# A stream-encoder step on one core: one half of a row factor summed one product later, and the last pair of heads' forms made on VectorE

## The chip, the cores and the metric

The kernel runs on one core of a Trainium2 chip, in one launch. The metric is device time in microseconds (us), the median of several executions. The engines have the profile's names: PE is TensorE (PEld its weight loads), DVE is VectorE, ACT is ScalarE, POOL is GpSimd, SP is SyncE. SP issues most of the DMA transfers; POOL and ACT issue some.

## The reference

One layer of an encoder runs on 512 prompt frames and 64 sample frames, 576 rows of width 2048. All of it is float32.

```python
hn = rmsnorm(x, g_norm1);  proj = hn @ w_in                 # 2048 -> 6144
q, k = rmsnorm per head;   o_attn = stick_breaking(q, k, v) # 8 heads of 128
u = gc * hc;  o_conv = gb * conv3_causal(u)                 # 1024 channels
mix = concat(rmsnorm(o_attn, g_attn_out), rmsnorm(o_conv, g_conv_out))
x = x + mix @ w_out
h2 = rmsnorm(x, g_norm2)
x = x + (silu(h2 @ w_gate) * (h2 @ w_up)) @ w_down          # 2048 -> 5632 -> 2048
```

## The kernel before

**Layout.** Activations lie with channels on the 128 partitions and the 576 frames along the row, in two halves of 288 (`HALVES`). A float32 operand is split into a rounded high part (a cast on ACT) and the rest (a subtraction on DVE, or on POOL where told so). `split` does both, at lines 222 and 223. A product of two such operands takes three matmuls, high by high, low by high, high by low, each 128x128 by 128x288.

**Products in sevens.** Most large products use seven block products in place of eight (numbered 1 to 7 in the code). Eight channel pairs and three matmuls make 24 matmuls for one block product. `prepare` makes the weight operand of a product four products ahead (a cast on ACT, a subtraction on DVE, and before it sums of weight blocks such as `s1`, written `s` in the profile, and differences in place in `raw_a` and `raw_b`). `multiply` issues the matmuls. `run` calls it and does what follows the product: `kept` copies a partial result out of PSUM on ACT while the same PSUM tile goes on collecting, and `finish` adds parts, multiplies by the row factor, and applies SiLU (gate) or the product with the gate (up).

**The feed-forward's start.** `order` lists the products. It begins

```python
order = [(0, 1), (0, 2), (1, 1), (1, 2), (0, 7), (0, 6), (0, 5), (0, 3), (0, 4), (1, 6), ...
```

with unit 0 the first gate block and unit 1 the first up block. Products 1, 6 and 3 of a unit collect in one PSUM tile, `psy`. After product 6 the copy `u2` is taken from it, and product 3 of the same unit must add to it only after that copy.

**The row factor.** RMSNorm's factor per frame, `R2`, is applied after the product, so the first products can start without it. The squares of the residual are summed over tiles in `acc2`; `split` makes `parts2`; `row_scale2` sums them over the partitions with two matmuls per half against a tile of ones (`channel_sums`, lines 470 and 471), and `rsqrt_mean` (lines 461 to 466) makes the factor with Ln and Exp on ACT and four steps on DVE. Its scratch tiles are shared: `ms` and `t` have one buffer each, and `kept` uses the same two tags, `ms` for the first copy of unit 1 and `t` for `u2`.

**The heads' forms.** The output projection's first units, for attention, take as frames seven combinations ("forms") of four blocks of a pair of heads. `head_forms` makes them for four pairs (k = 0 to 3): forms 1 to 3 are the blocks themselves, forms 5, 7, 6 and 4 are differences made in place on POOL (line 558). `put` splits each into one of eight stage tiles in turn and SP stores it. The low part of forms 5 and 6 is made on POOL, of the others on DVE. This is work in the background, stepped by `pipe.tick()` after each channel pair of a product; pairs 2 and 3 are the tile `o_ob`, the stage tiles are `hf`. It ends while the first products in sevens of the input projection begin (`conv_run`, line 1036, whose weights are `raw_a` and `raw_c`, whose evacuations are line 1060).

**Order of the work.** Each engine runs its own instructions in order. A scheduler decides that order when the program is built, from its own estimates; stretches of it are fixed by hand for some engines. So a change at one place can move instructions nearby on every engine.

Of the kernel before, what the change touches and what calls it, by code (L numbers as in the profile page):

```python
# [13 lines left out]
ALU = mybir.AluOpType  # L14
# [6 lines left out]
HALF = T // 2  # L21
HALVES = ((0, HALF), (HALF, T))
D = 2048
KD = D // P
NH = 8
# [69 lines left out]
def tile_hybrid_stream_step(  # L95
# [6 lines left out]
    nc = tc.nc  # L102
# [118 lines left out]
    def split(hi, lo, src, lo_eng=None):  # L221
        nc.scalar.copy(out=hi, in_=src)  # L222
        (lo_eng or nc.vector).tensor_tensor(out=lo, in0=src, in1=hi.bitcast(F32), op=ALU.subtract)  # L223

    def parts(name):
        t = tmp.tile([P, 2, HALF], F32R, tag="hl", name=name)
        return t[:, 0], t[:, 1]
# [32 lines left out]
    def misc(name):  # L260
        return ps_z.tile([P, 512], F32, tag="misc", name=name, bufs=2)
# [111 lines left out]
    with tc.manual_schedule(engines={mybir.EngineType.Activation, mybir.EngineType.DVE, mybir.EngineType.SP}):  # L373
# [26 lines left out]
        for kt in range(KD + LAG):  # L400
# [21 lines left out]
            if kt == 16:  # L422
                nc.vector.tensor_tensor(out=lo1[:, :1024], in0=raws[1][:, :1024], in1=hi1[:, :1024].bitcast(F32),  # L423
                                        op=ALU.subtract)
# [43 lines left out]
    def channel_sums(src_hi, src_lo, a, b, name):  # L468
        ps = misc(name)[:, : b - a]
        mm(ps, oner, src_hi, start=True, stop=False)  # L470
        mm(ps, oner, src_lo, start=False, stop=True)
        return ps
# [54 lines left out]
    def head_forms():  # L527

        turn = [0]
        two = [parts("sqg") for _ in HALVES]
        for (sh, sl), (a, b) in zip(two, HALVES):
            split(sh, sl, acc_a[:, a:b])
        yield 6
        for (sh, sl), (a, b) in zip(two, HALVES):
            rsqrt_mean(acc_a[:, a:b], channel_sums(sh, sl, a, b, "ssg"), 8 * P, HALF)
            yield 4
        for k in range(NH // 2):
            pair = o_half[k // 2][:, 2 * (k % 2) : 2 * (k % 2) + 2, :]  # L540
            four = pair.rearrange("p k (i t) -> p (k i) t", i=2)
            b11, b12, b21, b22 = (four[:, q, :] for q in range(4))
            for r in range(2):
                nc.vector.scalar_tensor_tensor(out=pair[:, r], in0=pair[:, r], scalar=col("ga", 2 * k + r), in1=acc_a,
                                               op0=ALU.mult, op1=ALU.mult)
            yield 2

            def put(f, src, lo_eng):
                t = bt["stage"][:, turn[0] % NP]
                turn[0] += 1  # L550
                split(t[:, 0], t[:, 1], src, lo_eng)
                nc.sync.dma_start(out=form_dram[f - 1, k].rearrange("f p t -> p f t"), in_=t.bitcast(F32))

            for f, src in ((1, b11), (2, b21), (3, b22)):
                put(f, src, nc.vector)
                yield 2
            for f, out, a, b in ((5, b11, b12, b11), (7, b12, b12, b22), (6, b22, b22, b11), (4, b21, b21, b22)):
                nc.gpsimd.tensor_tensor(out=out, in0=a, in1=b, op=ALU.subtract)
                yield 1
                put(f, out, nc.gpsimd if f in (5, 6) else nc.vector)  # L560
                yield 2
            if k == 1:
                bt["raw"] = apool.tile([P, 2048], F32, tag="oa", name="raw_c")
                assert cwanted[0] == (1, 0)
                call_columns([2])
# [970 lines left out]
    def run(n, p_):  # L1536
        st = unit[n]
        kind, fp = UNITS[n][:2]

        def kept(tag):  # L1540
            t = tmp.tile([P, HALF], F32, tag=tag, name="part", bufs=1)
            nc.scalar.copy(out=t, in_=st["y"])  # L1542
            return t

        def done(c, i, ps, part=None):
            if kind != "down":
                finish(kind, fp, c, i, ps, part)
            elif n in last:
                store_y(n, c, i)

        def add(c, i, ps, part=None):

            if kind != "down":
                return
            if n in first:
                if part is not None:
                    nc.vector.tensor_tensor(out=acc[fp, c, i], in0=ps, in1=part, op=ALU.add)
                else:
                    nc.scalar.copy(out=acc[fp, c, i], in_=ps)
                return  # L1560
            if ps is not None:
                nc.vector.tensor_tensor(out=acc[fp, c, i], in0=ps, in1=acc[fp, c, i], op=ALU.add)
            if part is not None:
                nc.gpsimd.tensor_tensor(out=acc[fp, c, i], in0=acc[fp, c, i], in1=part, op=ALU.add)

        if kind == "down" and p_ == 1 and n in first:
            take_blocks(fp)
        later = n not in first
        if p_ == 1:
            st["y"] = ps_pj.tile([P, HALF], F32, tag="pj", name="psy")  # L1570
            multiply(st["y"], n, 1, True)
            st["p1"] = kept("ms" if n else "acc")
        elif p_ == 2:
            x = misc("psx3")[:, :HALF] if n == 1 else ps_z.tile([P, 512], F32, tag="z0", name="psx2")[:, :HALF]
            multiply(x, n, 2, True)
            if n == 0:
                row_scale2()
            add(0, 0, x, st["p1"])
            done(0, 0, x, st["p1"])
        elif p_ == 6:  # L1580
            multiply(st["y"], n, 6, False)
            st["u2"] = kept("ms" if n == NGU - 1 else "t")
            if later:
                add(1, 0, None, st["u2"])
        elif p_ == 7:
            st["w"] = ps_z.tile([P, 512], F32, tag=f"z{n % 2 + 1}", name="psw")[:, :HALF]
            multiply(st["w"], n, 7, True)
            if later:
                add(1, 1, st["w"])
        elif p_ == 5 and n == 0:  # L1590

            x = misc("psx5")[:, :HALF]
            multiply(x, n, 5, True)
            st["p5"] = tmp.tile([P, HALF], F32, tag="acc", name="part5", bufs=1)
            nc.scalar.copy(out=st["p5"], in_=x)
            u4 = tmp.tile([P, HALF], F32, tag="ms", name="part", bufs=1)
            nc.gpsimd.tensor_tensor(out=u4, in0=st["p5"], in1=st["u2"], op=ALU.add)
            done(1, 1, st["w"], u4)
        elif p_ == 5:
            multiply(st["y"], n, 5, False)  # L1600
            u4 = kept("acc")
            add(1, 1, None if later else st["w"], u4)
            done(1, 1, st["w"], u4)
        elif p_ == 3:
            multiply(st["y"], n, 3, False)
            add(0, 1, st["y"])
            done(0, 1, st["y"], st.get("p5"))
        else:
            multiply(st["w"], n, 4, False)
            add(1, 0, st["w"], None if later else st["u2"])  # L1610
            done(1, 0, st["w"], st["u2"])
# [3 lines left out]
    first, last = {v[0] for v in visits.values()}, {v[-1] for v in visits.values()}  # L1615
# [166 lines left out]
    R2 = rpool.tile([P, T], F32, tag="R", name="R2", bufs=2)  # L1782
    parts2 = []
# [2 lines left out]
        split(sh, sl, acc2[i])  # L1786
        parts2.append((sh, sl))

    def row_scale2():
        for i, (a, b) in enumerate(HALVES):  # L1790
            ss = channel_sums(*parts2[i], a, b, "ss2")
            rsqrt_mean(R2[:, a:b], ss, D, HALF)

    for k_ in range(2, AHEAD):
        prepare(*order[k_])
    for k_, (n, p_) in enumerate(order):
        if (n, p_) == (NGU - 1, 1):
            hold.append(True)
            mode.enter_context(tc.manual_schedule(engines={mybir.EngineType.Activation, mybir.EngineType.DVE,
                                                           mybir.EngineType.SP, mybir.EngineType.Pool}))  # L1800
        run(n, p_)
        if k_ + AHEAD < len(order):
            prepare(*order[k_ + AHEAD])
        if k_ == 2:
            for t, j0, j1 in zip(late["b22"], (1, 0), (NP, 1)):
                nc.sync.dma_start(out=t.bitcast(F32), in_=b22_dram[j0:j1].rearrange("j f p t -> p (j f) t"))
        for p in turned.get((n, p_), ()):
            if p == "w":
                load_columns(one=True)
            else:  # L1810
                load_pair(p)
        if (n, p_) == (NGU - 1, 4):
            pairs.append(6)
            since = -16
            hold.clear()
            load_columns()
        if n >= NGU:
            pairs += calls[n - NGU] if p_ == 4 else ()
            since += UNITS[n][3]
            if pairs and since >= PACE:  # L1820
                load_pair(pairs.pop(0))
                since = 0
        if p_ == 2:
            for d in residual.get(n, ()):
                add_residual(d)
# [39 lines left out]
```

## Time and profile before

| what | value |
|---|---|
| time, median of 3 | 2369.54 us (2368.44 to 2373.28) |
| profiled execution | 2369.07 us, its span 2367.0 us |
| granted TensorE clock | 1.00 |
| PE busy | 99% of the span |
| DVE, ACT, POOL busy | 82%, 49%, 12% |

The profile has several views. The page gives busy time by engine. The waits say who waited for whom. The timeline lists instructions in order: start in us from the span's start, length in us, engine, line, operation, output<-inputs, sizes, how many were merged (xN), and in brackets the idle time before and who ended it. The chain is the work that ended last, followed backwards.

### The profile page before, as it was taken

To read this page: it belongs to the slowest core of one execution; us is meant where nothing else is said; L and a number is where in the kernel's file an instruction comes from. 1 tells how busy PE (TensorE), PEld (TensorE's weight loads), DVE (VectorE), ACT (ScalarE), POOL (GpSimd) and SP (SyncE) were. 2 spreads that over 40 slices of the span, in tenths; PEclk is the share of its full clock that TensorE was granted. 3 is DMA by queue.
4 is the path that set the end of the run, shared out by engine and by line. 5 is a ranking of instruction groups with operands and counts; after the bars stand their busy time and mean duration, and the time that the engine had idled before them with its cause. 6 is when DMAs were issued, how large, how long until landed. Compare 5 with 4: busy or idle time off the path is not lost.

```text
span 2367.0 us, 43888 instructions
## 1 busy us (share of the span) xinstructions
PE 2340.9 (99%) x17581; PEld 2329.5 (98%) x17581; DVE 1935.3 (82%) x2908; ACT 1156.0 (49%) x2039; POOL 294.5 (12%) x386
## 2 busy tenths in 40 slices
PE   8999999999999999999999999999999999999998
PEld 8999999999999999999999999999999999999998
DVE  7878777788887889888888888888888777887896
ACT  6656655444444555444444444444444444444443
POOL 1011111341111230000000000000000002431221
PEclk9999999999999999999999999999999999999999
DMA  8466544684368654444444444444444936885553
GB/s 259 128 175 169 139 138 112 217 266 126 110 226 227 194 166 154 137 152 136 139 152 135 140 152 134 141 152 133 142 152 132 356 115 208 221 235 199 190 143 85
DMA packets 588804, 395.74 MB, mean 167 GB/s; under 512 B 100030, under 2 KB 577720, under 8 KB 588600
## 3 DMA queue, kind: packets, MB, share of 16 engines
q1 hardware_dynamic: 574776, 375.93, 50.9%
q0 software_dynamic: 8624, 16.22, 3.4%
q8 instruction: 137, 2.24, 0.4%
q10 hardware_dynamic: 5200, 0.79, 0.2%
q14 instruction: 67, 0.55, 0.1%
HBM read 301.45 MB, written 91.44 MB: 166 GB/s over the span
## 4 chain that ended last, share of the span: by engine, by line
PE 89%; DVE 5%; DMA 2%; ACT 2%; issue 1%; POOL 0%; ACTq 0%; SPq 0%; POOLq 0%; DVEq 0%
PE psy L1532 33%; PE psw L1532 16%; PE pj L213 13%; PE psx L1532 8%; PE psy L1036 6%; PE pjo L213 4%; PE psw L1036 3%; PE psx L1036 2%; DVE whl L223 1%; DMA raw_a<-in_w_down_dram 1%; PE po L747 1%; PE z L679 1%; ACT whl L222 0%; PE os L777 0%; DVE whl L1008 0%
## 5 line engine op out<-in xcount | busy, mean ns | idle before, releaser
L1532 PE MATMUL psy<-h_s,whl 128*128 128x288 f32 x2787 | 411.7, 294 | 1.7 <-ACT part L1542 1.7
L213 PE MATMUL pj<-x,whi 128*128 128x288 f32 x1856 | 390.5, 297 | 0.3 <-DVE x L356 0.3
L1532 PEld LDWEIGHTS psy<-h_s,whl 128*128 128x128 f32 x2787 | 383.5, 188 | 2.6 <-ACT part L1542 2.6
L223 DVE TENSOR_TENSOR whl<-raw_a,whl 128x1024 fp32r<-128x1024 f32 (+4 forms) x296 | 318.3, 1076 | 57.3 <-ACT whl L222 55.6
L1532 PE MATMUL psw<-t,whl 128*128 128x288 f32 x2400 | 346.9, 294 | 0.0
L1532 PEld LDWEIGHTS psw<-t,whl 128*128 128x128 f32 x2400 | 327.6, 188 | 0.0
L222 ACT CAST whl<-raw_a 128x1024 fp32r<-128x1024 f32 (+4 forms) x296 | 267.6, 906 | 116.7 <-issue 35.3
L213 PEld LDWEIGHTS pj<-x,whi 128*128 128x128 f32 x1856 | 305.0, 189 | 1.0 <-DVE x L356 0.6
L213 PE MATMUL pj<-x,wlo 128*128 128x288 f32 x928 | 274.5, 296 | 0.1
L223 DVE TENSOR_TENSOR whl<-raw_b,whl 128x1024 fp32r<-128x1024 f32 (+5 forms) x190 | 198.1, 1042 | 68.6 <-ACT whl L222 67.2
L222 ACT CAST whl<-raw_b 128x1024 fp32r<-128x1024 f32 (+5 forms) x190 | 164.9, 871 | 169.6 <-issue 73.1
L1542 ACT COPY part<-psy 128x288 f32<-128x288 f32 x242 | 96.7, 400 | 281.9 <-PE psy L1532 258.4
L1532 PE MATMUL psy<-t2t,whl 128*128 128x288 f32 x1212 | 183.5, 295 | 1.2 <-ACT part L1542 1.2
L1532 PE MATMUL psy<-b22m,whl 128*128 128x288 f32 x1212 | 183.1, 295 | 0.6 <-ACT part L1542 0.6
L213 PEld LDWEIGHTS pj<-x,wlo 128*128 128x128 f32 x928 | 174.9, 188 | 0.7 <-DVE wlo L423 0.3
L1532 PE MATMUL psx<-h_s,whl 128*128 128x288 f32 x1185 | 173.7, 294 | 0.0
L1532 PEld LDWEIGHTS psy<-t2t,whl 128*128 128x128 f32 x1212 | 168.3, 188 | 1.6 <-ACT part L1542 1.4
L1532 PEld LDWEIGHTS psy<-b22m,whl 128*128 128x128 f32 x1212 | 168.1, 188 | 0.9 <-ACT part L1542 0.9
L1532 PEld LDWEIGHTS psx<-h_s,whl 128*128 128x128 f32 x1185 | 162.7, 188 | 0.0
L222 ACT CAST whl<-s 128x1024 fp32r<-128x1024 f32 (+5 forms) x81 | 72.2, 892 | 101.7 <-PE psw L1532 99.4
L1311 POOL DMA_DIRECT2D hid_dram<-form x3 | 2.3, 751 | 947.2 <-DVE form L223 947.2
L1532 PE MATMUL psy<-t,whl 128*128 128x288 f32 x576 | 106.5, 294 | 0.0
(456 smaller groups left out, 4392.5 us busy)
## 6 DMA issues: line engine op xcount, KB each, us to landing
hid_dram<-form SPq DMA_DIRECT2D x147, 288.0 KB, 2.3
raw_a<-in_w_in_dram SPq DMA_DIRECT2D x41, 1024.0 KB, 6.1
raw_a<-in_w_gate_dram SPq DMA_DIRECT2D x22, 1024.0 KB, 6.1
raw_a<-in_w_up_dram SPq DMA_DIRECT2D x22, 1024.0 KB, 5.9
raw_b<-in_w_gate_dram SPq DMA_DIRECT2D x22, 1024.0 KB, 6.7
raw_b<-in_w_up_dram SPq DMA_DIRECT2D x22, 1024.0 KB, 7.0
h_s<-hid_dram SPq DMA_DIRECT2D x10, 2016.0 KB, 12.2
raw_a<-in_w_out_dram SPq DMA_DIRECT2D x16, 1024.0 KB, 5.5
```

Of the source, the lines that this page charges most:

```text
L213: mm(ps, w_[:, k, csl], x_, start=(k == 0 and n == 0), stop=(k == nk - 1 and n == 2))
L222: nc.scalar.copy(out=hi, in_=src)
L223: (lo_eng or nc.vector).tensor_tensor(out=lo, in0=src, in1=hi.bitcast(F32), op=ALU.subtract)
L679: mm(zb[i], a_[:, kk], b_[:, q0:TP], start=(n == 0), stop=False, skip_group_check=True)
L747: mm(po[:, i * P : 512], a_[:, i, :], b_[:, : 512 - i * P], stop=(i == 0 and n == 2), **kw)
L1036: mm(ps, whl[:, w_, j, :], x_, start=(start and j == 0 and q == 0), stop=(j == m - 1 and q == 2), skip_group_check=True)
L1311: q.dma_start(out=hid_dram[fp][2 * n - 2 : 2 * n].rearrange("f p t -> p f t"), in_=t.bitcast(F32))
L1532: mm(ps, whl[:, w_, j, :], x_, start=(start and j == 0 and q == 0), stop=(j == len(xs_) - 1 and q == 2), skip_group_check=True)
L1542: nc.scalar.copy(out=t, in_=st["y"])
```

## The change

Two edits. First, `row_scale2` works on one half at a time. The first half is made where both were, after product (0, 2) is issued; the second half is made after product (1, 1). Second, for the last pair of heads (k = 3) the four differences and the low parts of forms 5 and 6 are issued on DVE; pairs 0 to 2 stay as they were.

```diff
             for f, out, a, b in ((5, b11, b12, b11), (7, b12, b12, b22), (6, b22, b22, b11), (4, b21, b21, b22)):
-                nc.gpsimd.tensor_tensor(out=out, in0=a, in1=b, op=ALU.subtract)
+                last = k == NH // 2 - 1
+                (nc.vector if last else nc.gpsimd).tensor_tensor(out=out, in0=a, in1=b, op=ALU.subtract)
                 yield 1
-                put(f, out, nc.gpsimd if f in (5, 6) else nc.vector)
+                put(f, out, nc.gpsimd if f in (5, 6) and not last else nc.vector)
...
             if n == 0:
-                row_scale2()
+                row_scale2(0)
...
-    def row_scale2():
-        for i, (a, b) in enumerate(HALVES):
-            ss = channel_sums(*parts2[i], a, b, "ss2")
-            rsqrt_mean(R2[:, a:b], ss, D, HALF)
+    def row_scale2(i):
+        a, b = HALVES[i]
+        ss = channel_sums(*parts2[i], a, b, "ss2")
+        rsqrt_mean(R2[:, a:b], ss, D, HALF)
...
         if k_ == 2:
+            row_scale2(1)
             for t, j0, j1 in zip(late["b22"], (1, 0), (NP, 1)):
```

## The prediction

> **What bounds the kernel now.** I read the page first.
>
> ```profile
> PE 2340.9 (99%) x17581; PEld 2329.5 (98%) x17581; DVE 1935.3 (82%) x2908; ACT 1156.0 (49%) x2039; POOL 294.5 (12%) x386
> ```
>
> PE is busy for 99% of the span, so only stretches in which PE stands still can change the time. The waits of PE say where those are (us in total, times, longest).
>
> ```profile
> PE psx_s L333 <- DMA xsn<-in_x_sample_dram: 5.7, 1, 5.7
> PE psy L1532 <- ACT part L1542: 3.5, 5, 1.2
> PE z L679 <- ACT kh L222: 2.0, 1, 2.0
> PE ss L470 <- ACT sq L222: 1.8, 2, 1.5
> ```
>
> The longest is the wait for the first input; after it no single wait is over 2.0. The one at line 470 holds, with its longest piece of 1.5, the row factor's sum, which the change moves. The forms have their waits at line 1036, where the products in sevens begin. The timeline gives each place its ceiling.
>
> At the forms, VectorE, GpSimd and TensorE:
>
> ```profile
> 481.83 0.81 DVE L223 TENSOR_TENSOR hf<-o_ob,hf 128x288 fp32r<-128x288 f32 x2
> ...
> 487.57 4.43 DVE L223 TENSOR_TENSOR hf<-o_ob,hf 128x288 fp32r<-128x288 f32 x1 [0.44 <-ACT hf L222]
> ...
> 492.37 1.23 DVE L1008 TENSOR_TENSOR whl<-raw_c,whl 128x1024 fp32r<-128x1024 f32 x1
> ...
> 497.84 0.45 DVE L1060 TENSOR_TENSOR cv<-psx,part 128x288 f32<-128x288 f32 x1
> ```
> ```profile
> 487.82 0.82 POOL L223 TENSOR_TENSOR hf<-o_ob,hf 128x288 fp32r<-128x288 f32 x1
> ...
> 490.88 0.80 POOL L223 TENSOR_TENSOR hf<-o_ob,hf 128x288 fp32r<-128x288 f32 x1
> ```
> ```profile
> 493.37 3.58 PE L1036 MATMUL psy<-x,whl 128*128 128x288 f32 x24
> 498.44 3.41 PE L1036 MATMUL psx<-x,whl 128*128 128x288 f32 x24 [1.48 <-DVE cv L1060]
> ...
> 502.44 0.79 PE L1036 MATMUL psw<-xs_t,whl 128*128 128x288 f32 x4 [0.46 <-DVE whl L1008]
> ```
>
> One low part on VectorE took 4.43 us. Two of the same size took 0.81 (0.45 and a step of 0.36). It was stuck from 487.57 to 492.00, while GpSimd ran five instructions without a gap, from 487.82 to 491.68 (the first and the last are shown). Behind it stand the split of raw_c (and a second one) and the evacuation cv, for which PE waits at 498.44.
>
> At the row factor, TensorE:
>
> ```profile
> 889.83 0.29 PE L471 MATMUL ss<-sq,oner 128*128 128x288 f32 x1
> 891.59 0.40 PE L470 MATMUL ss<-sq,oner 128*128 128x288 f32 x1 [1.47 <-ACT sq L222]
> 892.15 0.40 PE L471 MATMUL ss<-sq,oner 128*128 128x288 f32 x1 [0.17 <-DVE sq L223]
> 892.39 0.43 PE L1532 MATMUL psy<-h_s,whl 128*128 128x288 f32 x2
> ...
> 898.77 3.33 PE L1532 MATMUL psw<-t,whl 128*128 128x288 f32 x24
> ...
> 908.29 0.57 PE L1532 MATMUL psy<-b22m1z,whl 128*128 128x288 f32 x3
> ```
>
> Three products of 24 matmuls run from 898.77 to 908.29: 3.17 us each, 0.13 a matmul. The two sums of the second half wait for its split, and product (1, 1) behind them starts at 892.39. Without that wait and with one sum pair less it would start at 889.83 + 0.13 = 889.96. The two sums (0.26) come later anyway, so 2.17 us is all that this edit can win. At the forms the ceiling is 502.44 - (493.37 + 2 x 3.17 + 0.13) = 2.60. Together that is 4.8 us, 0.2% of the time. A difference of 0.2%, 4.7 us, is about what a measurement of this kernel can tell from no change. So a gain that shows would need both ceilings whole.
>
> **Part one: the forms of the last pair.** The order of the changed program's instructions shows four subtractions and two low parts gone from GpSimd and standing on VectorE among the same neighbours; ScalarE's, SyncE's and TensorE's orders around them are as before. The same stores go out of SyncE's queue in the same order, and nobody else waits for GpSimd there. VectorE pays 6 x 0.36 = 2.2 us. It saves the stuck 4.43 - 0.45 = 3.98, since of GpSimd's five instructions only the sum acc_c stays. That leaves 1.8. Two of GpSimd's subtractions lay earlier, beside other steps of VectorE, for which I add an estimated 0.2. Net: the split at 492.37 comes some 2.0 us earlier, as do cv at 497.84 and the split that frees psw at 502.44. PE no longer waits at psx (it arrives at 493.37 + 3.17 = 496.54, cv is done at 496.3), and at psw it still waits some 0.5. **Gain 2.0 us.** Bounds: 2.6, the ceiling, and 0, if VectorE was held by something else than GpSimd (a rival, below). A loss would need VectorE to be late by more than before, and it has 1.8 us in hand.
>
> **Part two: the second half one product later.** PE's sums for it now stand behind (1, 1) at 893.1, when their input is there (by 892.15, where PE waited for it): the 2.17 us go. What is late next? The rows of VectorE and ScalarE around it:
>
> ```profile
> 896.52 1.22 DVE L223 TENSOR_TENSOR whl<-raw_b,whl 128x1024 fp32r<-128x1024 f32 x1
> ```
> ```profile
> 901.17 1.28 ACT L1379 ACT_TABLE_LOAD   x1
> 902.46 0.45 ACT L1379 ACTIVATE gs<-gs 128x288 f32<-128x288 f32 x1
> ...
> 905.31 0.40 ACT L1542 COPY part<-psy 128x288 f32<-128x288 f32 x1
> ...
> 909.89 1.05 ACT L222 CAST whl<-raw_b 128x1024 fp32r<-128x1024 f32 x1 [1.01 <-DVE raw_b L1476]
> ```
>
> First, product (0, 7) (psw, 898.77) needs the split at 896.52. VectorE, not PE, sets that: the chain ahead of raw_a doesn't move (it waits for the same casts and for the first half's Ln and Exp), and in the changed order two short instructions (the gate's first sum, and the first factor) stand ahead of raw_a. So the split moves by 2 x 0.36 to 897.25 and ends at 898.47. PE would now arrive at 889.96 + 2 x 3.17 + 0.26 = 896.56; it waits 1.9 us and goes on at 898.50. **Of the 2.17 us, 0.27 are left.**
>
> Second, the scratch. The mean square of the second half now takes the tile ms after unit 1's first copy, so it must wait until that copy has been added, after (1, 2). Ln and Exp then fall behind the gate's SiLU on ScalarE, and the changed program has three more table loads there: ahead of Ln, ahead of Exp, and for the next SiLU. And u2 takes the tile t after the factor's last step. In the program before, u2's copy (905.31) stands ahead of the gap; in the changed one its place on ScalarE is: two weight casts, load, Ln, cast of a form, load, Exp, copy of psx, cast of raw_b, then u2. Product (0, 3), before at 908.29, may not add to psy until u2 is read.
>
> The sum. (0, 7) ends at 898.50 + 3.17, its result is there at some 901.9, and the first cast waits for that (its weight tile). Two casts of 1.05, overlapping by 0.1: 903.8. Load 1.28, Ln 0.45, the form's cast 0.4 (as the copy), load 1.28, Exp 0.45: 907.5 with overlaps of 0.1. VectorE waits there in its order: 0.36, the next s1 1.14 (1.22 less its overlap), 0.36, and raw_b's difference 1.22: 910.7 with the handovers. The cast of raw_b (1.05) and the copy (0.40) follow: u2 is read at 912.1. PE arrives at 898.50 + 3 x 3.17 = 908.0 and stands for 4.1 us. (0, 3) starts at 912.1 instead of 908.29: **a loss of 3.8 us**, the 0.27 counted in. Bounds: 2.5 (the two loads partly under waits) and 4.5 (each of ten handovers 0.07 longer). Behind it, GpSimd's sum for (0, 5) and VectorE's gate steps come 4 us late too, but so does PE, whose next operands, for (1, 6), are needed only at 912.1 + 2 x 3.17 = 918.4; some 3 us of VectorE steps stand ahead of them. The waits of PE list nothing from 960 to 1900 us, so nothing absorbs the shift.
>
> Here a rule differs from a row. The load row is 1.28 us and the activation behind it starts at 902.46, 0.01 after it ends. The Trainium skill, ScalarE: Activation LUTs, "What ACT_TABLE_LOAD costs", adds a drain of about 1.38 us to each switch; no such gap stands at this row. With it, two loads on the path would add 2.8 us to the sum below, 2374.1. The sum goes by the row.
>
> **The sum.** 3.8 - 2.0 = +1.8 us. Against the profiled execution, 2369.07 (span 2367.0), that is 2370.9. The median lies 0.47 above it: **2371.3 us**, own range 2369.8 to 2372.8 from the bounds of both parts.
>
> **Rivals.**
>
> *The array cools in the new stall (slower).* The new stall, 4.1 us, is longer than any before but the 5.7 at the start, and after it matmuls of the same size are slow:
>
> ```profile
> 11.14 0.44 PE L213 MATMUL pj<-x,wlo 128*128 128x288 f32 x1
> 11.38 0.68 PE L213 MATMUL pj<-x,whi 128*128 128x288 f32 x2
> ...
> 15.66 0.29 PE L213 MATMUL pj<-x,wlo 128*128 128x288 f32 x1
> 15.79 0.43 PE L213 MATMUL pj<-x,whi 128*128 128x288 f32 x2
> ```
>
> Their step is 0.24 at 11 us and 0.13 at 15.7. If that comes back, product (0, 3) costs 24 x 0.11 = 2.6 more: 2373.9. It passes +0.2% once more than (4.7 - 1.8) / 0.11 = 27 matmuls are slow; two products give 2376.6. Against it: one stall at the very start is a cold start, not a stall. The Trainium skill, TensorE: Matmul & The Clock Gate, "Why this matters for your kernels", warns of idle gaps over about 3 us; by that rule this rival holds, and the trace has no such gap after the start to test it. Chance 0.18.
>
> *The stuck low part was waiting for a store.* The chain names the store between it and what follows:
>
> ```profile
> 488.67 3.21 DMA form_dram<-hf
> ```
>
> That transfer lands at 491.88, just when VectorE goes on. Then VectorE would stay stuck and only the 2.2 us move onto it: no gain at the forms, +3.8, 2373.3. Against it: its row names ScalarE's cast, not a store, as what it waited for, and the five GpSimd instructions end at nearly the same moment. Chance 0.12.
>
> *The table loads hide.* If both run while ScalarE would wait anyway, u2 comes 1.3 to 2.6 earlier: 2368.7 to 2370.0. For it: ScalarE has idle time there. Against it: the loads stand in the order between instructions that wait for each other. Chance 0.10.
>
> **How the numbers follow.** The forecast has 0.60, the rivals 0.18, 0.12 and 0.10. Faster by over 0.2% (under 2364.8) needs both ceilings whole and no stall at u2: 0.03. Slower by over 0.2% (over 2374.3): the longer half of the cooling case, 0.09, the store case with the loss at its upper bound of 4.5 or cooled as well, 0.06, and handovers longer than that bound allows in the forecast's own case, 0.05: 0.20. The rest, 0.77, is within. The range 2368.4 to 2374.8 holds the forecast, the hidden loads, the store case and the cooling of one product; outside lie the longer cooling and both ceilings whole.
>
> **What would show it.** At the forms: no VectorE instruction of 4 us, psx without a wait, psw at a time 2 us earlier. At the factor: no wait at line 470 in unit 0's start, a wait of psw for VectorE's whl of about 1.9, and a wait of psy for ScalarE's part of about 4 in (0, 3), with three table loads ahead and around it. Steps of 0.13 behind it say the array stayed warm, 0.24 that it cooled. If PE does not wait at (0, 3), the forecast is wrong, and the time falls below 2368.

## The result, and the profile after

| kernel | median | runs | profiled execution, its span |
|---|---|---|---|
| before | 2371.64 us (2368.44 to 2374.80) | 20 | 2369.07 us, 2367.0 us |
| changed | 2375.28 us (2372.54 to 2378.42) | 20 | 2375.91 us, 2374.0 us |

The changed kernel takes 1.0017 times as long (95% interval 1.0011 to 1.0024); its median is 3.6 us higher. The ratios here and below are estimated from all runs and need not equal the quotient of the medians, which is 1.0015 here. The kernel before, run beside it, is 2.1 us above the median of the three runs known at first.

The page's busy line and the waits of PE, after:

```profile
PE 2341.5 (99%) x17581; PEld 2329.6 (98%) x17581; DVE 1937.0 (82%) x2914; ACT 1159.0 (49%) x2042; POOL 286.4 (12%) x380
```
```profile
PE psy L1533 <- ACT part L1543: 6.8, 4, 4.2
...
PE psw L1533 <- DVE whl L223: 1.6, 1, 1.6
PE psx L1037 <- DVE cv L1061: 1.4, 1, 1.4
```

Six instructions have moved from POOL to DVE and ACT has three more, the table loads. The two waits at lines 470 and 471 in the factor are gone. In their place stand a wait of 1.6 us (psw for VectorE's weight) and one of 4.2 us (psy for the copy on ScalarE), the longest after the start.

The timeline of PE at the row factor, after, from the first half's sums to product (0, 4):

```profile
892.06 0.29 PE L471 MATMUL ss<-sq,oner 128*128 128x288 f32 x1
...
900.68 3.31 PE L1533 MATMUL psw<-t,whl 128*128 128x288 f32 x23 [1.59 <-DVE whl L223]
...
907.40 2.94 PE L1533 MATMUL psx<-h_s,whl 128*128 128x288 f32 x21
...
914.49 0.67 PE L1533 MATMUL psy<-b22m1z,whl 128*128 128x288 f32 x3 [4.15 <-ACT part L1543]
914.99 4.48 PE L1533 MATMUL psy<-b22m,whl 128*128 128x288 f32 x21
919.31 3.33 PE L1533 MATMUL psw<-t,whl 128*128 128x288 f32 x24
```

Product (0, 3) starts at 914.49, 22.43 us after the first half's second sum; before it was 908.29 - 889.83 = 18.46. That is 3.97 us later. Then it takes 919.31 - 914.49 = 4.82 us, where the three products behind each other in the profile before took 3.17 each. So 1.65 us more go inside the product, and not in a wait: no view of waits lists them. The windows show why. The number ahead of the DMA share is the clock that TensorE was granted:

```profile
914.50:915.20 0.70, 0.70 (x5) 0.70 (x6) 0.70 (x2) 0.61 (x1) 0.69 (x1) 1.00 1.10 331
915.30:918.50 3.20, 3.20 (x15) 3.20 (x15) 2.51 (x5) 1.74 (x3) 1.06 (x1) 0.50 0.04 11
918.70:919.30 0.60, 0.60 (x6) 0.60 (x6) 0.60 (x1) 0.13 (x1) 0.00 (x0) 1.00 0.00 0
```

The product begins at full clock, the clock falls to 0.50 some 0.8 us later, and it is back at 1.00 after about 3.4 us. In the 3.2 us of the middle line the matmuls start 0.24 us apart, about 13 of them (the 15 of the row are all that touch it); at a step of 0.13 it would be 24.

ScalarE ahead of u2's copy (914.04), after:

```profile
906.10 1.28 ACT L462 ACT_TABLE_LOAD   x1
907.40 0.45 ACT L462 ACTIVATE y<-ms 128x288 f32<-128x288 f32 x1
...
908.18 1.28 ACT L463 ACT_TABLE_LOAD   x1
909.48 0.45 ACT L463 ACTIVATE y<-y 128x288 f32<-128x288 f32 x1
...
913.09 1.05 ACT L222 CAST whl<-raw_b 128x1024 fp32r<-128x1024 f32 x1 [2.32 <-DVE raw_b L1477]
914.04 0.39 ACT L1543 COPY part<-psy 128x288 f32<-128x288 f32 x1
```

Ln, Exp, their loads, the cast that waits 2.32 us for VectorE's difference, then the copy: the chain of the prediction. Each activation starts within 0.02 us of its load's end.

At the forms, PE and ScalarE, after:

```profile
486.14 3.33 PE L1037 MATMUL psy<-x,whl 128*128 128x288 f32 x24
...
494.43 3.34 PE L1037 MATMUL psy<-x,whl 128*128 128x288 f32 x23 [0.86 <-DVE whl L1009]
499.22 3.46 PE L1037 MATMUL psx<-x,whl 128*128 128x288 f32 x24 [1.44 <-DVE cv L1061]
...
503.16 3.31 PE L1037 MATMUL psw<-xs_t,whl 128*128 128x288 f32 x23 [0.35 <-DVE whl L1009]
```
```profile
487.30 0.43 ACT L222 CAST hf<-o_ob 128x288 fp32r<-128x288 f32 x1 [5.12 <-DMA form_dram<-hf]
```

From the first row to the last it is 17.02 us, against 502.44 - 487.02 = 15.42 before (the first start, 487.02, is a row of that profile not shown). So in this execution the forms cost 1.6 us instead of bringing 2. The 5.12 us wait of a cast for the store of its stage tile was 2.61 in the profile before.

### The profile page after: what moved, and what is told of

Its sections match the earlier page's. It is cut to its first block, busy times and chain, and to the rows that moved or that the text cites. A ratio compares the mean times of both kernels' runs of the same rounds, so it can differ in the third digit from the quotient of the medians.

```text
span 2374.0 us, 43890 instructions
## 1 busy us (share of the span) xinstructions
PE 2341.5 (99%) x17581; PEld 2329.6 (98%) x17581; DVE 1937.0 (82%) x2914; ACT 1159.0 (49%) x2042; POOL 286.4 (12%) x380
## 4 chain that ended last, share of the span: by engine, by line
PE 87%; DVE 5%; DMA 3%; ACT 3%; issue 1%; POOL 0%; ACTq 0%; SPq 0%; POOLq 0%; DVEq 0%
PE psy L1533 33%; PE psw L1533 16%; PE pj L213 12%; PE psx L1533 8%; PE psy L1037 6%; PE pjo L213 4%; PE psw L1037 3%; PE psx L1037 1%; DVE whl L223 1%; DMA raw_a<-in_w_out_dram 1%; ACT whl L222 1%; PE po L748 1%; PE z L680 1%; DMA raw_b<-in_w_down_dram 1%; DMA form_dram<-hf 0%
```

## The experiments

Two stretches of PE's timeline carry the comparison, because they leave out what differs between executions elsewhere. Each comes from one profiled execution, the median from all runs; the changed kernel's +7.2 is to be held against the 7.0 us between the two profiled spans, not against its median. One is the forms' stretch just used. The other is the factor's: from the second sum of the first half to the start of (0, 4), 911.46 - 889.83 = 21.63 us before and 27.25 after. Differences of the median are against runs of the kernel before that were measured beside it, with the interval of the ratio in us. All times are in us.

| kernel | forms' stretch | factor's stretch | both, against before | median, against before |
|---|---|---|---|---|
| before | 15.42 | 21.63 | | |
| changed | 17.02 | 27.25 | +7.2 | +3.6 (2.6 to 5.7) |
| changed, again | 14.26 | 28.15 | +5.4 | +4.2 (2.8 to 6.9) |
| forms_only | 13.87 | 21.67 | -1.5 | -2.8 (-4.7 to -0.5) |
| row_only | 15.42 | 28.82 | +7.2 | +5.4 (2.4 to 6.4) |
| row_warm | 15.37 | 25.71 | +4.0 | +3.5 (1.2 to 5.2) |
| after_warm | 13.84 | 25.68 | +2.5 | +3.2 (0.7 to 5.0) |
| row_own_r | 15.41 | 23.33 | +1.7 | +2.0 (-0.9 to 3.3) |
| row_before_copy | 15.42 | 22.85 | +1.2 | -0.2 (-2.4 to 1.9) |
| both_before_copy | 13.83 | 22.82 | -0.4 | +0.6 (-1.9 to 2.4) |

forms_only, row_only, row_warm and row_before_copy shared 33 runs of the kernel before on one chip (2371.77); after_warm, row_own_r, both_before_copy and the changed kernel's second row shared another 33 on a second chip (2370.26).

**The forms alone.** The factor as before, the forms as changed.

```diff
             if n == 0:
-                row_scale2(0)
+                row_scale2()
...
-    def row_scale2(i):
-        a, b = HALVES[i]
-        ss = channel_sums(*parts2[i], a, b, "ss2")
-        rsqrt_mean(R2[:, a:b], ss, D, HALF)
+    def row_scale2():
+        for i, (a, b) in enumerate(HALVES):
+            ss = channel_sums(*parts2[i], a, b, "ss2")
+            rsqrt_mean(R2[:, a:b], ss, D, HALF)
...
         if k_ == 2:
-            row_scale2(1)
```

> The last pair's forms on VectorE, the row factor as before. Theory A: 0 to 2 us faster than the kernel before, since VectorE is no longer held by GpSimd for 4 us. Rival B: 1 to 2 us slower, with ScalarE's casts of the forms waiting for the stores of their stage tiles. Rival C: within 0.5 us, because the stores set the end of the forms either way.

Measured: 2369.02 us (2367.48 to 2371.36), ratio 0.9989 (0.998 to 0.9998). PE, and VectorE beside GpSimd, in this kernel:

```profile
495.55 3.45 PE L1037 MATMUL psx<-x,whl 128*128 128x288 f32 x24 [0.24 <-DVE cv L1061]
...
499.49 3.33 PE L1037 MATMUL psw<-xs_t,whl 128*128 128x288 f32 x23 [0.36 <-DVE whl L1009]
```
```profile
486.20 1.42 DVE L223 TENSOR_TENSOR hf<-o_ob,hf 128x288 fp32r<-128x288 f32 x1
```
```profile
486.47 0.82 POOL L510 TENSOR_TENSOR acc_c<-acc_c,sqm 128x288 f32<-128x288 f32 x1
```

The wait at psx fell from 1.48 to 0.24. One GpSimd instruction is left, and the low part beside it takes 1.42 us in place of 4.43. The forms bring 1.55 us in this stretch; the median shows a gain as large or larger.

**The factor alone.** The forms as before, the factor as changed.

```diff
-                last = k == NH // 2 - 1
-                (nc.vector if last else nc.gpsimd).tensor_tensor(out=out, in0=a, in1=b, op=ALU.subtract)
+                nc.gpsimd.tensor_tensor(out=out, in0=a, in1=b, op=ALU.subtract)
...
-                put(f, out, nc.gpsimd if f in (5, 6) and not last else nc.vector)
+                put(f, out, nc.gpsimd if f in (5, 6) else nc.vector)
```

> The row factor's second half moved, the forms left on GpSimd. Theory A (the whole loss is the late copy u2 and a cooled array): 5 to 6 us slower than the kernel before (in the changed kernel's profile (0, 3) starts some 3.8 us late and its 24 matmuls take 1.65 more), a wait of psy for ScalarE's part of about 4, and (0, 3) at 4.8 us instead of 3.2. Rival B (the forms on VectorE cost the time, as the first products in sevens came 1.6 us late in that profile): at most 4 us slower here, and the rest shows with the forms alone.

Measured: 2377.22 us (2372.31 to 2380.27), ratio 1.0019 (1.001 to 1.0027). The stuck low part is back:

```profile
489.58 4.41 DVE L223 TENSOR_TENSOR hf<-o_ob,hf 128x288 fp32r<-128x288 f32 x2 [0.83 <-ACT hf L222]
```

The row merges two; the first, alone, took 4.04 us, from 489.58 to 493.62, while GpSimd ran five instructions without a gap to 493.29. So it is GpSimd's sequence that holds VectorE. The ends fit: the held instruction ends 0.32 to 0.33 us after GpSimd's last in the kernel before (492.00 and 491.68), here, and with the forms alone (487.62 and 487.29). PE's products at the factor, and the windows of the same kernel:

```profile
903.34 4.67 PE L1532 MATMUL psw<-t,whl 128*128 128x288 f32 x23 [1.81 <-DVE whl L223]
907.81 3.18 PE L1532 MATMUL psy<-t2t,whl 128*128 128x288 f32 x21
...
918.50 1.09 PE L1532 MATMUL psy<-b22m1z,whl 128*128 128x288 f32 x3 [3.94 <-ACT part L1542]
...
923.31 3.33 PE L1532 MATMUL psw<-t,whl 128*128 128x288 f32 x24
```
```profile
903.40:904.80 1.40, 1.40 (x11) 1.40 (x12) 1.40 (x3) 1.39 (x2) 0.00 (x0) 1.00 0.06 20
904.90:908.10 3.20, 3.20 (x16) 3.20 (x15) 3.20 (x5) 0.08 (x1) 0.00 (x0) 0.50 0.00 0
```

The array cooled twice here, that is, the clock fell to 0.50. (0, 3) took 4.81 us. And (0, 7), behind a wait of only 1.81 us, took 907.81 - 903.34 = 4.47 for 23 matmuls, where the changed kernel's took 903.83 - 900.68 = 3.15 after 1.59 (903.83 is a row not shown). The clock was still 1.00 for about 1.5 us of work behind that gap, and then 0.50 for some 3.4. This profiled execution was the kernel's slowest, 2380.27 us, so its stretch in the table is longer than the median's difference.

**Keeping the array busy in the stall.** The factor alone, with 30 matmuls ahead of (0, 3) whose result nobody uses.

```diff
+    WARM = 30
...
         elif p_ == 3:
+            if n == 0:
+                idle = misc("idle")[:, :HALF]
+                for q in range(WARM):
+                    mm(idle, oner, h2a[0][0], start=True, stop=True, skip_group_check=True)
             multiply(st["y"], n, 3, False)
```

> As the row factor alone, and 30 matmuls (some 4 us) into a spare PSUM tile, whose result is not used, ahead of product (0, 3), in the gap in which PE would stand still. Theory A (the array cools in the gap): 1.6 us faster than the row factor alone, (0, 3) back to 3.2 us with a step of 0.13, although PE issues more. Rival D (the slow (0, 3) has another cause, its weights or the second wait): no faster, (0, 3) still at 4.8.

Measured: 2375.29 us (2372.35 to 2376.82), ratio 1.0014 (1.0005 to 1.0022), 1.9 less than the factor alone, though the two intervals overlap. PE in this kernel:

```profile
915.61 0.66 PE L1532 MATMUL psy<-b22m1z,whl 128*128 128x288 f32 x3
...
918.92 3.33 PE L1532 MATMUL psw<-t,whl 128*128 128x288 f32 x24
```

(0, 3) takes 3.31 us. The start is as late as before, the slow matmuls are gone.

**The same in the changed kernel.** The same 30 matmuls added to the changed kernel.

> The changed kernel with 30 unused matmuls on TensorE ahead of product (0, 3), which fill the stall. If the cooled array is the term that the prediction left out: the wait of 4.15 us is gone, product (0, 3) takes 3.2 us instead of 4.8, and the time falls by 1.6 us against the changed kernel, to about 2373.5; what is left above the kernel before is the start of (0, 3), 3.8 us later, less the forms' 2. If the slow matmuls had another cause than the idle array: (0, 3) still takes 4.8 us and the time is that of the changed kernel or up to 0.3 us more.

Measured: 2373.46 us (2370.58 to 2376.57), ratio 1.0012 (1.0003 to 1.0021); the changed kernel, measured beside it, had 2374.49, 1.0 more. PE and its window:

```profile
911.91 0.66 PE L1533 MATMUL psy<-b22m1z,whl 128*128 128x288 f32 x3
...
915.21 3.33 PE L1533 MATMUL psw<-t,whl 128*128 128x288 f32 x24
```
```profile
911.90:915.20 3.30, 3.29 (x24) 3.29 (x25) 2.60 (x4) 2.34 (x2) 1.84 (x1) 1.00 0.22 66
```

24 matmuls at clock 1.00. The time fell by less than the 1.6 us expected; the two intervals overlap, so this pair does not size the effect, the product's own length does. The mean granted clock of the executions measured together points the same way: 0.9981 over 11 of the changed kernel, 0.9993 over 11 with the unused matmuls, 0.9991 over 33 of the kernel before. So the array cools in the changed kernel's executions in general, not in the profiled ones only, and the lost 0.0010 of 2374 us, 2.4 us, is an estimate of the most that it costs on average, since a part can lie in the stall.

**The second half summed before unit 1's first copy.** The forms as before. The sums still come after the matmuls of (1, 1), but ahead of the copy that takes the tile ms.

```diff
             multiply(st["y"], n, 1, True)
+            if n == 1:
+                row_scale2(1)
             st["p1"] = kept("ms" if n else "acc")
...
-            row_scale2(1)
```

> The second half is summed behind product (1, 1) as in the change, but its factor is asked for before unit 1's first copy takes the scratch tile, so Ln and Exp come before the gate's SiLU and u2 keeps its place. Theory A: the wait at (0, 3) shrinks from 4 us to under 1.5 and no array cools; the time is within 1.5 us of the kernel before (the wait of psw for VectorE's split, 1.6, remains). Rival E (PE's late sums alone cost the time, not the scratch): still 4 us or more slower.

Measured: 2371.55 us (2369.98 to 2374.67), ratio 0.9999 (0.999 to 1.0008). ScalarE's u2 copy and PE in this kernel:

```profile
908.85 0.40 ACT L1542 COPY part<-psy 128x288 f32<-128x288 f32 x1 [1.16 <-DVE R L466]
```
```profile
909.30 0.67 PE L1532 MATMUL psy<-b22m1z,whl 128*128 128x288 f32 x3 [0.72 <-ACT part L1542]
...
913.17 3.47 PE L1532 MATMUL psw<-t,whl 128*128 128x288 f32 x24 [0.40 <-DVE gs L1376]
```

The wait of (0, 3) is 0.72 us in place of 4. The order has the same three table loads. Ln and Exp stand earlier on ScalarE, though still behind the gate's SiLU and not ahead of it as expected, and u2's copy starts 18.5 us after the first half's second sum (890.32 in this profile) in place of 22.0.

**Scratch tiles of its own.** The factor alone, at the place of the change, with two other tiles for the second half's mean square and its square.

```diff
-        rsqrt_mean(R2[:, a:b], ss, D, HALF)
+        own = [tmp.tile([P, HALF], F32, tag=tag, name=tag + "2") for tag in ("r", "sq")] if i else (None, None)
+        rsqrt_mean(R2[:, a:b], ss, D, HALF, *own)
```

> The row factor's edit alone (heads' forms as before), with the second half's mean square and its square in two scratch tiles of their own, not in those that the copies of unit 1 and u2 use. The built order has the same three table loads; u2's copy stands earlier on ScalarE, behind one weight cast fewer and no longer behind raw_b's difference and the factor's last steps on VectorE. If the scratch tiles' order makes the stall: the wait of (0, 3) for ScalarE's part is under 1 us; a later wait takes part of it back, 1.5 to 3 us for the weight split that now stands behind the factor's steps on VectorE, at (0, 4) or (1, 6); 2372 to 2375 us. If the table loads and their place behind SiLU make it whatever the tiles: (0, 3) still waits 3 us or more for part, cools, and the time is that of the factor's edit alone, about 2377.

Measured: 2372.29 us (2369.75 to 2374.12), ratio 1.0005 (0.9996 to 1.0014). ScalarE's u2 copy and PE:

```profile
909.56 0.39 ACT L1542 COPY part<-psy 128x288 f32<-128x288 f32 x1
```
```profile
912.24 0.53 PE L1532 MATMUL psy<-b22m1z,whl 128*128 128x288 f32 x2 [1.17 <-DVE whl L223]
...
915.85 3.47 PE L1532 MATMUL psw<-t,whl 128*128 128x288 f32 x24 [0.31 <-DVE gs L1376]
```

(0, 3) no longer waits for u2, though the three more table loads are there. The wait of 4 us was made by the shared tiles. What is late next is the split of the weight for (0, 3), 1.17 us, expected at 1.5 to 3 at the products behind it; it came one product earlier and smaller.

**Both, with the better place.** The changed kernel with the second half summed before unit 1's first copy.

> The changed kernel with its forms on VectorE, and the second half of the row factor made in run 1 of unit 1, between the product and its first copy, instead of after it. If the two parts simply add up: the forms' gain (2.75 us when alone) with no loss at the factor (0.2 us less than before when alone): 2368 to 2370 us, 2 to 3 us below the kernel before, and (0, 3) begins with a wait under 1 us at full step (24 matmuls in about 3.2 us). If the forms' gain exists only in some executions (the store that their stage tile waits for), or the factor's part costs something that the other run hid: 2371 to 2373, no difference from the kernel before.

Measured: 2370.89 us (2367.14 to 2372.57), ratio 1.0001 (0.9992 to 1.001). PE at the forms and at the factor:

```profile
501.56 3.30 PE L1037 MATMUL psw<-xs_t,whl 128*128 128x288 f32 x23 [0.36 <-DVE whl L1009]
...
908.30 0.66 PE L1533 MATMUL psy<-b22m1z,whl 128*128 128x288 f32 x3 [0.71 <-ACT part L1543]
...
912.17 3.44 PE L1533 MATMUL psw<-t,whl 128*128 128x288 f32 x24 [0.44 <-DVE gs L1377]
```

The expected 2 to 3 us of gain did not come out. The stretches say why the expectation was too high: the factor's is 1.19 us longer than before, the forms' 1.59 shorter, so 0.4 is left, and the median's interval holds that. The experiment on the factor alone had shown no loss in the median, but its stretch had shown 1.2.

**The changed kernel once more.** No edit.

> The changed kernel once more, unchanged, for a second profile of the same program. If the 5.1 us that ScalarE's cast of a form waited for the store of its stage tile are a chance of that one execution: here the wait is 1 to 3 us, PE arrives at the second psw of the forms' window 2 us or more earlier against its first product of sevens there, and the profiled time is lower by that. If the forms on VectorE bring that wait themselves: 4 to 6 us again. In both cases the stall of about 4 us at (0, 3) and its slow matmuls are there again, with the same numbers within 0.3 us; the median is 2374 to 2376.

Measured: 2374.49 us (2372.38 to 2377.68), ratio 1.0021 (1.0012 to 1.0029). PE, ScalarE, and the windows:

```profile
504.08 2.12 PE L1037 MATMUL psw<-xs_t,whl 128*128 128x288 f32 x14 [0.40 <-DVE whl L1009]
...
914.23 1.09 PE L1533 MATMUL psy<-b22m1z,whl 128*128 128x288 f32 x3 [4.14 <-ACT part L1543]
...
919.93 3.37 PE L1533 MATMUL psw<-t,whl 128*128 128x288 f32 x24
```
```profile
488.22 0.43 ACT L222 CAST hf<-o_ob 128x288 fp32r<-128x288 f32 x1 [3.80 <-DMA form_dram<-hf]
```
```profile
912.90:914.20 1.30, 0.00 (x0) 0.00 (x0) 1.30 (x2) 1.27 (x2) 0.00 (x0) 0.50 1.15 348
914.20:919.60 5.40, 5.37 (x22) 5.38 (x23) 4.33 (x6) 2.77 (x3) 1.84 (x1) 0.50 0.12 36
```

The store wait is 3.80 us, above the 1 to 3 expected of chance and below the 4 to 6 of a fixed cost, and the forms' stretch is 14.26: it gains 1.16. The three other kernels with the forms on VectorE gain 1.55 to 1.59. The first profile's loss there is the exception among five. The stall is 4.14 again. But (0, 3) takes 5.70 us and not 4.8, outside the 0.3 us that was expected: the clock had fallen at about 912.8, still in the stall, and stayed at 0.50 until about 919.65.

## Why the prediction was wrong

**The base.** The prediction added 1.8 us to 2369.54, the median of three runs. Twenty runs give 2371.64. Of the 4.0 us between the forecast 2371.3 and the result, 2.1 are this. The forecast's +1.8 compares with a measured +3.6. Its own range was also narrower than its bounds: 2.5 - 2.6 to 4.5 - 0 around the same base give 2369.4 to 2374.0, not 2369.8 to 2372.8.

**Part one, the forms: right in mechanism.** The forecast was 2.0 us; four of five profiles give 1.2 to 1.6 in the stretch, and the median of the forms alone 2.8 (0.5 to 4.7). The low part was held by GpSimd, as assumed: it shrinks to 1.42 us where those instructions go and returns at 4.04 where they come back. PE still waits 0.24 at psx with the forms alone, where none was forecast. The store rival had the wrong engine but a real wait behind it: ScalarE's cast waited 2.6 to 3.5 us for a store in the five profiles with the forms as before, 2.8 to 5.1 in the five with the edit, and the one execution with 5.1 lost the gain. That the store took it was not tested, nor why the store was late there.

**Part two, the waits: right.** Left of the 2.17 us were 0.32 (psw at 8.62 us after the first half's second sum, against 8.94), forecast 0.27; psw waits 1.59, forecast 1.9. (0, 3) starts 3.97 and 3.99 us later in the two profiles, forecast 3.8; its wait is 4.15, forecast 4.1. The three table loads are there, at 1.28 us each, and the two ahead of u2 have no gap behind them (0.02 us), so the row was the right choice. The drain that the Trainium skill, ScalarE: Activation LUTs, "What ACT_TABLE_LOAD costs", adds to each switch does not show there. The cause named, scratch tiles shared with unit 1's copy and with u2, is shown by the two experiments that loosen it: the stretch is 1.2 and 1.7 us longer than before in place of 5.6, with the same three loads. So the loads alone do not make the stall.

**Part two, the step that failed.** The forecast let (0, 3) run at 0.13 us a matmul behind the stall and so put the cooled array at nothing in its sum; the rival in which it cools had a chance of 0.18. It is what happens: the step is 0.24, the sign that the prediction named. Its first argument, that only stretches in which PE stands still can change the time, missed the same thing, for this loss lies inside a product. With 4.82 - 3.17 = 1.65 us and 5.70 - 3.17 = 2.53 in the two profiles, the prediction's sum becomes 3.8 - 2.0 + 1.65 = +3.5 to +4.3; measured were +3.6 and +4.2. That close a match is partly luck, since by the stretches the 2.0 was high. With the 1.5 of the forms alone and the late start of 4.0 the sum is +4.1 to +5.0, inside both intervals. The experiments with the unused matmuls show that idleness is the cause: same late start, 3.3 us for the product, clock 1.00. The reason given against the rival, that the slow start of the program was a cold start and not a stall, did not hold. Its price was of the right size, 2.6 for one product at half step, but it isn't fixed: the clock stays at 0.50 for a stretch of its own length, and what of that lies in the stall costs nothing.

That stretch is 3.41 us in the changed kernel and twice in the factor alone (behind the 1.81 us gap and at (0, 3)), and 6.83, twice as long, in the second profile of the changed kernel. The Trainium skill, TensorE: Matmul & The Clock Gate, "What's actually happening", tells of a free-running window of 3.4 us after which the gate is set anew from how busy the array was. The stretches agree with that length and with a start that doesn't follow the gap (the last section works this out). Its rule in "Why this matters for your kernels", gaps over about 3 us, held for the stall. It would have spared the 1.81 us gap, where the clock fell all the same; there the measurement decides.

**The range.** 2368.4 to 2374.8 had room for the cooling of one product, but on the low base; from 2371.64 the cooling rival's 4.4 us would have given 2376.0.

## What to carry to other kernels

Moving a reduction later is not free of where its scratch lives: list what else uses each scratch tile, since a shared one can put a copy that the matmuls wait for behind the whole chain. Price a new TensorE stall as the stall plus up to one or two slow stretches behind it; read the granted clock in fine windows, since the waits don't list this. Read it beside the step of the matmuls, too: in the profile before it is 1.00 from 10 to 15.5 us, where the step is 0.24 at first. A prediction of a few us should not rest on three runs. Of all versions run, only the one with the forms alone was faster than the kernel before, 0.9989 (0.998 to 0.9998).

## What the runs showed of the hardware that was not expected

A gap of 1.81 us cooled the array in one execution; gaps of 1.54 to 1.70 us at the same place in seven others did not. The kept profiles say more than the experiments asked. In all ten, PE waits 2.02 to 2.06 us for ScalarE (kh) near 70 us, and in six of them, not in the profile before, the clock is 0.50 near there for 3.41 us. So the length of a gap alone doesn't decide.

Its position does. Every stretch at 0.50 lasts 3.41 us or twice that. In the factor alone the second and third begin 13.65 us apart, 4 x 3.4133, and the first, at 72.01, lies 832.85 = 244 x 3.4133 us ahead of the second; in the second profile of the changed kernel the two lie 839.68 = 246 x 3.4133 apart. So in these traces the clock is set anew on a fixed grid of 3.4133 us. Laid through the falls of the seven profiles that have one, the grid gives PE's busy time in each of its windows. The factor alone, then the changed kernel, each with the window behind it (its length, PE's busy time, and the clock ahead of the DMA share):

```profile
901.45:904.86 3.41, 1.60 (x12) 1.00 0.58 203
904.87:908.27 3.40, 3.40 (x16) 0.50 0.00 0
```
```profile
898.19:901.60 3.41, 1.82 (x14) 1.00 0.56 198
901.61:905.01 3.40, 3.40 (x27) 1.00 0.00 0
```

Past the start of the program (first 8 us), every window at full clock with 1.81 us or more of idle time is followed by half clock (ten windows), and none with 1.74 or less is, of some 4800. The limit thus lies at about half a window, by the profile's modelled ends of matmuls. A window already at half clock is kept there by less: 1.40 us of idle time did it in the second profile. An estimate from this: a stall over some 3.6 us always cools the array, since one of two windows gets half of it or more; one between 1.8 and 3.6 cools it by chance of position.

VectorE's subtractions of one size (0.45 us otherwise) took 4.0 to 4.5 us beside five GpSimd instructions without a gap, and 1.42 to 1.79 beside a single one of 0.82. They ended about 0.3 us after GpSimd's last.
